# Gate and up column pairs of an FFN computed token-major, their h turned by DMA

## The chip, the cores and the metric

One core of a Trainium2 chip (trn2) runs the whole program in one launch. The metric is the device time of a launch in microseconds (us); the kernel before takes 912.5 us (median of three runs, 911.65 to 912.99).

## The reference

Two decoder layers work on 256 tokens of width 1024. Each layer is an FFN, a mixer and a second FFN, each between two RMSNorms, with the result added to the residual. Only the FFN is touched by the change:

```python
def _rmsnorm(x, g):
    x32 = x.astype(jnp.float32)
    y = x32 * lax.rsqrt(jnp.mean(x32 * x32, axis=-1, keepdims=True) + RMS_EPS)
    return y.astype(x.dtype) * g

def _swiglu(h, wg, wu, wd):
    return (jax.nn.silu(h @ wg) * (h @ wu)) @ wd
...
for l in range(DEPTH):
    f = _swiglu(_rmsnorm(h, ff1_norm_pre[l]), ff1_w_gate[l], ff1_w_up[l], ff1_w_down[l])
    h = h + 0.5 * _rmsnorm(f, ff1_norm_post[l])
    m = _hybrid_mixer(...)
    h = h + _rmsnorm(m, mix_norm_post[l])
    f = _swiglu(_rmsnorm(h, ff2_norm_pre[l]), ff2_w_gate[l], ff2_w_up[l], ff2_w_down[l])
    h = h + 0.5 * _rmsnorm(f, ff2_norm_post[l])
```

The FFN's hidden width is 2816, everything is float32.

## The kernel before

**Arithmetic.** A float32 product runs on TensorE as three products: each operand x is split into hi, rounded to the format fp32r (ScalarE, lines L114 for weights and L250 for activations), and lo = x - hi (VectorE, L115 and L251), and hi·hi + lo·hi + hi·lo is summed in PSUM. `xT` holds the normed input turned, that is with the 1024 features on partitions in eight blocks `k` and the 256 tokens on the free axis; `both` holds its hi and lo side by side. t is the tile of 128 tokens, 0 or 1.

**Units.** The 2816 hidden columns are eleven units of 256, numbered 0 to 10. Units 0 and 1 are `FIRST`; (2, 3), (5, 6) and (8, 9) are `QUADS`, computed together by a scheme with seven products; 4, 7 and 10 are `PAIRS`, computed one at a time by `ffn_pair`. There are four FFNs, so twelve pairs. After a unit's hidden activation h has been made and turned (`hT`), its share of the down projection is `down(i, t)`: twelve matmuls of 512 columns into the two PSUM banks `acc[t]` (L412), for t = 0 and t = 1. I write (10, 0) for `down` of unit 10 and tile 0. Of the last four units (7 to 10, `TAIL`) the t = 0 parts come first and the t = 1 parts after them, so that the norms of tile 0 run while TensorE does tile 1.

**A pair before.** `ffn_pair` calls `mm_side` for gate and then for up. Weights stand still and the input streams: the result is feature-major, so h needs no turning. For each half j of 128 features, eight matmuls stream `both`, 512 columns (L359), and eight stream hi alone, 256 columns, with the weights' lo (L361); so a pair is 32 matmuls of 512 columns and 32 of 256. ScalarE copies the second half of the bank out (L364), VectorE adds the first (L365), four times a pair; then silu (L541), the product (L544) and the split of h (L250, L251).

**The other units** are token-major: the input stands still, the weights stream 512 columns (L390, L559), and h comes out with tokens on partitions. To turn it, `send` parts the float32 words into 16-bit halves (ScalarE, L510) and issues a DMA transpose on SyncE's queue (L514), and `receive` joins them again (ScalarE, L522) and splits them (L250, L251). In some places `turn_tile` turns on TensorE instead (L533). Within a pair, `turn()` receives one tile of the quad before it and `take()` the other.

**End of an FFN.** `post(0)` norms acc[0] and adds it to h (ScalarE L258 and L260, GpSimd L263, VectorE L275 and L282); `pre_scale` norms h for the next stage (L258, L260, L263, L291), and `pre_turn` turns the result on TensorE, two times four transposes (L301). The last FFN has nothing after it but the output. Weights come by DMA on SyncE's queue (L85) into five raw buffers, and are split into five pairs of hi and lo buffers. `pump()` loads and splits ahead as buffers allow; `W.allowed` limits how many loads it may issue.

**Order.** The program is recorded in the order of the code, and the framework then sets each engine's own order by its estimates of when things are ready; `issue_after` and `keep_in_program_order` bind it. All engines but TensorE's weight loads run their queue strictly in that order.

## Time and profile before

| | |
|---|---|
| Timed runs, median (lowest, highest) | 912.5 (911.65, 912.99) us |
| Profiled execution, span on the chip | 910.8 us |
| Granted TensorE clock, mean | 0.999 |
| DMA: bytes moved, mean rate | 198.63 MB, 218 GB/s |
| Packets under 512 B | 35858 of 60880 |

The profiled execution is given by its span, first to last instruction; the timed runs' median lies 1.7 us above it. Busy times are unions, so that overlapping instructions count once; a row of a group gives the line, the engine, the operation, the tiles it writes and reads, the count, then busy us and the mean ns of one, then idle time before it with its releaser. PE is TensorE, ACT ScalarE, DVE VectorE, POOL GpSimd, SP SyncE. A matmul's own duration of 0.39 us overlaps the next; what counts is the spacing from one start to the next.

### The profile page before, as it was taken

How to read it: one execution, taken by the hardware profiler on the slowest of the kernel's cores; microseconds unless marked ns; L12 is line 12 of the kernel's file. 1: busy time of each engine (PE TensorE's matmuls, PEld its weight loads, DVE VectorE, ACT ScalarE, POOL GpSimd, SP SyncE). 2: the span in 40 equal slices, each digit the busy share in tenths (PEclk: the TensorE clock that was granted, in tenths of full speed). 3: DMA queues.
4: the chain of work that ended last, by engine and by line, in shares of the span. 5: the costliest groups of instructions: out<-in, count | busy, mean ns of one | idle time of the engine just before them, and what ended most of it. 6: DMA issues, size and time to landing. Idle time of an engine off the chain costs nothing.

```text
span 910.8 us, 12262 instructions
## 1 busy us (share of the span) xinstructions
PE 901.0 (99%) x4556; PEld 760.6 (84%) x4556; DVE 801.6 (88%) x1068; ACT 665.9 (73%) x1045; POOL 29.8 (3%) x49
## 2 busy tenths in 40 slices
PE   8999999999999999999999999999999999999997
PEld 5888888889988888888888888888998888888885
DVE  6999988789878999988899999988989699999983
ACT  7776776778858777776878768767797668768772
POOL 0000000000001000000000000000000110000000
PEclk9999999999999999999999999999999999999999
DMA  9677977765355587768755968695824256978641
GB/s 360 181 274 227 384 188 282 251 214 204 78 195 208 128 314 205 289 162 288 244 187 149 339 196 299 173 305 200 298 109 162 93 173 180 323 214 298 177 124 47
DMA packets 60880, 198.63 MB, mean 218 GB/s; under 512 B 35858, under 2 KB 36370, under 8 KB 38804
## 3 DMA queue, kind: packets, MB, share of 16 engines
q1 hardware_dynamic: 58948, 185.13, 58.5%
q0 software_dynamic: 1728, 12.58, 7.3%
q8 instruction: 36, 0.59, 0.2%
q14 instruction: 24, 0.20, 0.1%
q10 hardware_dynamic: 144, 0.13, 0.0%
HBM read 188.65 MB, written 1.05 MB: 208 GB/s over the span
## 4 chain that ended last, share of the span: by engine, by line
PE 92%; DVE 5%; issue 2%; DMA 1%; ACT 0%; POOLq 0%; SPq 0%; POOL 0%; DVEq 0%
PE acc L412 29%; PE wk L559 23%; PE wk L390 13%; PE wk L359 9%; PE wk L350 6%; PE wk L361 5%; DVE lo L115 3%; PE wk L377 1%; PE wk L301 1%; DMA raw<-in_ff_f 1%; PE wk L1084 1%; PE acc L827 0%; DVE raw L113 0%; PE acc L897 0%; PE acc L1032 0%
## 5 line engine op out<-in xcount | busy, mean ns | idle before, releaser
L115 DVE TENSOR_TENSOR lo<-raw,hi 128x1024 fp32r<-128x1024 f32 (+2 forms) x452 | 464.3, 1076 | 37.4 <-ACT hi L114 36.8
L114 ACT ACTIVATE hi<-raw 128x1024 fp32r<-128x1024 f32 (+2 forms) x452 | 398.7, 937 | 72.2 <-DVE raw L113 30.1
L412 PE MATMUL acc<-hi,t 128*128 128x512 f32 x832 | 214.7, 391 | 0.0
L412 PEld LDWEIGHTS acc<-hi,t 128*128 128x128 f32 x832 | 155.0, 188 | 31.4
L412 PE MATMUL acc<-lo,t 128*128 128x512 f32 x416 | 113.4, 390 | 0.0
L559 PE MATMUL wk<-hi,n 128*128 128x512 f32 x384 | 100.5, 390 | 0.0
L390 PE MATMUL wk<-hi,xT 128*128 128x512 f32 x384 | 98.9, 393 | 0.2
L359 PE MATMUL wk<-xT,hi 128*128 128x512 f32 x384 | 95.9, 392 | 0.0
L412 PEld LDWEIGHTS acc<-lo,t 128*128 128x128 f32 x416 | 77.9, 188 | 16.3
L390 PEld LDWEIGHTS wk<-hi,xT 128*128 128x128 f32 x384 | 71.0, 188 | 16.4 <-ACT hi L114 1.6
L559 PEld LDWEIGHTS wk<-hi,n 128*128 128x128 f32 x384 | 71.8, 188 | 14.8
L359 PEld LDWEIGHTS wk<-xT,hi 128*128 128x128 f32 x384 | 69.8, 189 | 13.0
L559 PE MATMUL wk<-hi,xT 128*128 128x512 f32 x288 | 77.6, 390 | 0.1
L113 DVE TENSOR_TENSOR raw<-raw,raw 128x1024 f32<-128x1024 f32 x56 | 67.2, 1215 | 0.0
L559 PEld LDWEIGHTS wk<-hi,xT 128*128 128x128 f32 x288 | 53.8, 188 | 11.3 <-DVE t L599 0.4
L361 PEld LDWEIGHTS wk<-xT,lo 128*128 128x128 f32 x384 | 52.4, 190 | 3.8
L361 PE MATMUL wk<-xT,lo 128*128 128x256 f32 x384 | 53.5, 282 | 0.0
L559 PE MATMUL wk<-lo,n 128*128 128x512 f32 x192 | 52.1, 390 | 0.0
L390 PE MATMUL wk<-lo,xT 128*128 128x512 f32 x192 | 52.0, 391 | 0.0
L510 ACT ACTIVATE t<-t 128x1024 uint16<-128x1024 uint16 x31 | 32.6, 1055 | 24.4 <-DVE t L630 16.2
L390 PEld LDWEIGHTS wk<-lo,xT 128*128 128x128 f32 x192 | 36.0, 188 | 8.3 <-DVE lo L115 0.8
L559 PEld LDWEIGHTS wk<-lo,n 128*128 128x128 f32 x192 | 36.0, 188 | 7.7 <-DVE lo L115 0.2
(184 smaller groups left out, 947.8 us busy)
## 6 DMA issues: line engine op xcount, KB each, us to landing
raw<-in_ff_q SPq DMA_DIRECT2D x48, 1024.0 KB, 6.4
raw<-in_ff_d SPq DMA_DIRECT2D x44, 1024.0 KB, 5.1
raw<-in_ff_f SPq DMA_DIRECT2D x16, 1024.0 KB, 7.1
raw<-in_ff_q POOLq DMA_DIRECT2D x12, 1024.0 KB, 8.0
raw<-in_ff_g SPq DMA_DIRECT2D x12, 1024.0 KB, 4.8
raw<-in_ff_u SPq DMA_DIRECT2D x12, 1024.0 KB, 4.8
raw<-in_w_in SPq DMA_DIRECT2D x10, 1024.0 KB, 5.3
raw<-in_w_kvz SPq DMA_DIRECT2D x8, 1024.0 KB, 6.1
```

The lines of the kernel that those rows point to most:

```text
L113: nc.vector.tensor_tensor(raw[:, s], self.raw[x][:, s], self.raw[y][:, s], op=op)
L114: self.act = nc.scalar.activation(hi[:, s], raw[:, s], AF.Copy)
L115: nc.vector.tensor_tensor(lo[:, s], raw[:, s], hi[:, s].bitcast(F32), op=ALU.subtract)
L301: pre_turn.last = nc.tensor.transpose(ps[:, k * P : (k + 1) * P], xn[i][:, k * P : (k + 1) * P], ident)
L350: nc.tensor.matmul(ps, w[:, k, s], y[:, k, :], start=i == 0 and k == 0, stop=i == 2 and k == KD - 1)
L359: nc.tensor.matmul(ps, hi[:, k, s], both[:, :, k, :], start=k == 0, stop=k == KD - 1)
L361: mm_side.end = nc.tensor.matmul(ps[:, S:], lo[:, k, s], xT[0][:, k, :], start=False, stop=k == KD - 1, skip_group_check=True)
L377: nc.tensor.matmul(ps, x[:, k, s], w[:, k, :], start=i == 0 and k == 0, stop=i == 2 and k == KD - 1)
L390: m = nc.tensor.matmul(ps, y[:, k, :], w[:, k, :], start=h == 0 and n == 0, stop=h == 1 and n == len(parts) - 1)
L412: m = nc.tensor.matmul(acc[b], x[:, j, s], w[:, j, b * 512 : (b + 1) * 512], start=first and j == 0 and i == 0, stop=last and j == 1 and i ...
L510: part = send.last = nc.scalar.activation(halves.rearrange("p (a n) -> p a n", a=2), x[:, :].bitcast(U16).rearrange("p (n a) -> p a n", a= ...
L559: nc.tensor.matmul(ps, x[:, k, :], w[:, k, :], start=first and n == 0, stop=n == len(parts) - 1, skip_group_check=not first)
```

## The change

A pair becomes token-major like the rest. Its weights are stored as two units of half of K each, with the 256 columns of gate and the 256 of up side by side. `half(k, t)` is twelve matmuls of 512 columns; the order is half 0 of both tiles, half 1 of tile 0, half 1 of tile 1, into two PSUM banks, one a tile. After `half(0, 1)` comes `turn()`, after `half(1, 0)` comes `take()`. Silu now reads the gate half of the bank and the product the up half. Then h is sent and received by DMA. For pairs 4 and 7 both tiles go in one transpose, which is received in `turn()` of the next quad. For pair 10 each tile has its own h, its own send of half the size and its own receive behind the pair; meanwhile `W.allowed = 0` holds loads back until the second of them has been issued. `send`, `receive` and the slicing in `mm_rows` take their size from the tile.

```diff
         def pair(i):
-            for k in "gu":
-                p[k, i] = W.plan(a[f"ff{n}_{k}"][l, PAIRS.index(i)])
+            for k in range(2):
+                p["p", i, k] = W.plan(a[f"ff{n}_p"][l, 2 * PAIRS.index(i) + k])
...
-    def ffn_pair(i, p, turn, take, by_dma):
-        s = mm_side(p["g", i], buf())
-        taken = mm_side.last
-        nc.scalar.activation(s, s, AF.Silu)
-        turn()
-        hf = mm_side(p["u", i], buf(), take)
-        nc.vector.tensor_tensor(hf, hf, s, op=ALU.mult)
-        hT = (buf(F32R), buf(F32R))
-        split_into(hT, (slice(None), slice(None)), hf)
-        if by_dma:
-            pump_behind(taken)
-        else:
-            W.pump()
-        return hT
+    def ffn_pair(i, p, turn, take):
+
+        by_tile = i == PAIRS[-1]
+        ps = [bank(), bank()]
+        hf = [buf(n=256) for _ in range(2)] if by_tile else buf()
+        sent = []
+
+        def half(k, t):
+            hi, lo = (w[:, :UNIT].rearrange("p (k n) -> p k n", k=4) for w in W.get(p["p", i, k]))
+            x = [y[:, 4 * k : 4 * k + 4, t * P : (t + 1) * P] for y in xT]
+            parts = [(c, n) for n in range(3) for c in range(4)]
+            for n, (c, part) in enumerate(parts):
+                y, w = ((x[0], hi), (x[0], lo), (x[1], hi))[part]
+                m = nc.tensor.matmul(ps[t], y[:, c, :], w[:, c, :], start=k == 0 and n == 0,
+                                     stop=k == 1 and n == len(parts) - 1)
+            return m
+
+        def gated(t):
+            s = buf(n=256)
+            nc.scalar.activation(s, ps[t][:, :256], AF.Silu)
+            if by_tile:
+                nc.vector.tensor_tensor(hf[t], ps[t][:, 256:], s, op=ALU.mult)
+                sent.append(send(hf[t]))
+            else:
+                s, u, o = (x.rearrange("p (j n) -> p j n", n=P) for x in (s, ps[t][:, 256:], hf))
+                nc.vector.tensor_tensor(o[:, t::2], u, s, op=ALU.mult)
+
+        half(0, 0)
+        mid = half(0, 1)
+        W.done(p["p", i, 0])
+        with tc.issue_after(mid.ins):
+            turn()
+        half(1, 0)
+        take()
+        gated(0)
+        ffn_pair.end = half(1, 1)
+        W.done(p["p", i, 1])
+        gated(1)
+        if not by_tile:
+            sent.append(send(hf))
+        if by_tile:
+            W.allowed = 0
+        pump_behind(mid)
+        if by_tile:
+            W.allowed = 10**6
+            pump_behind(send.dma)
+        return sent
...
             def turn():
+                if sent:
+                    hT[before[0]] = receive(sent.pop())
                 if not hf:
                     return
...
-        for b in before:
-            both(b)
+        hT[NU - 1] = {0: receive(sent[0]), "at": 0}
+        both(NU - 1)
         post(0, acc[0], gain, before_next if last else None)
         xn0 = None if last else before_next(0)
+        hT[NU - 1][1] = receive(sent[1])
         for i in range(NU - TAIL, NU):
```

How the orders move, at three places. `hi41` and `lo41` are the down weights of unit 10 in the first FFN, `hi36` those of unit 7, `hi40` those of unit 9; acc62 and acc63 are acc[0], acc64 and acc65 acc[1]. L412 of before is L393 now.

TensorE at the end of the first FFN, before: (9, 0) ends, then one matmul of (7, 1) and the twelve of (10, 0).

```order
L412 MATMUL acc63_507<-hi40_1387,t125_1450 128x512
L412 MATMUL acc65_521<-hi36_1306,t107_1143 128x512
L412 MATMUL acc62_506<-hi41_1503,t132_1499 128x512 x2
L412 MATMUL acc62_506<-lo41_1504,t132_1499 128x512 x2
L412 MATMUL acc62_506<-hi41_1503,t133_1500 128x512 x2
L412 MATMUL acc63_507<-hi41_1503,t132_1499 128x512 x2
L412 MATMUL acc63_507<-lo41_1504,t132_1499 128x512 x2
L412 MATMUL acc63_507<-hi41_1503,t133_1500 128x512 x2
L412 MATMUL acc64_520<-hi36_1306,t107_1143 128x512
L412 MATMUL acc65_521<-hi36_1306,t107_1143 128x512
```

Now, same place (the rows before these are six more of (7, 1), behind the end of (9, 0)):

```order
L393 MATMUL acc64_520<-lo36_1273,t113_1203 128x512
L393 MATMUL acc65_521<-lo36_1273,t113_1203 128x512
L393 MATMUL acc64_520<-hi36_1272,t114_1204 128x512
L393 MATMUL acc62_506<-hi41_1451,t141_1497 128x512 x2
L393 MATMUL acc62_506<-lo41_1452,t141_1497 128x512 x2
L393 MATMUL acc62_506<-hi41_1451,t142_1498 128x512 x2
L393 MATMUL acc63_507<-hi41_1451,t141_1497 128x512 x2
L393 MATMUL acc63_507<-lo41_1452,t141_1497 128x512 x2
L393 MATMUL acc63_507<-hi41_1451,t142_1498 128x512 x2
L393 MATMUL acc65_521<-hi36_1272,t114_1204 128x512
```

Nine matmuls of (7, 1) stand in front of (10, 0) now, and three are left behind it. The second and third FFN end alike; in the fourth (10, 0) follows the twenty-four of (8, 0) and (9, 0) at once, as before.

TensorE at the transposes of `pre_turn`, first FFN, before: they come when (9, 1) is done. wk152 and wk153 are the two banks they fill, n150 and n151 the halves of the normed input.

```order
L412 MATMUL acc64_520<-hi40_1387,t130_1476 128x512
L412 MATMUL acc65_521<-hi40_1387,t130_1476 128x512
L301 MATMUL wk152_1629<-ident_82,n150_1589 128x128 x4
L301 MATMUL wk153_1636<-ident_82,n151_1590 128x128 x4
L412 MATMUL acc64_520<-hi41_1503,t132_1499 128x512 x2
```

Now:

```order
L393 MATMUL acc64_520<-hi40_1353,t133_1422 128x512
L393 MATMUL acc65_521<-hi40_1353,t133_1422 128x512
L393 MATMUL acc64_520<-hi41_1451,t162_1549 128x512 x2
L301 MATMUL wk164_1589<-ident_82,n159_1543 128x128 x4
L393 MATMUL acc64_520<-lo41_1452,t162_1549 128x512
L301 MATMUL wk165_1596<-ident_82,n160_1544 128x128 x4
```

Two matmuls of (10, 1) have slid in front of the first four transposes, one more in front of the second four. Between the last matmul of (10, 0) and the first transpose there stand 29 matmuls now (3, 24 and 2), 34 before.

ScalarE behind the weight splits in the last pair of the fourth FFN, before. t888 and t893 are joined halves of quad (8, 9), tiles 0 and 1; L364, L541 are the copies and the silu of the pair.

```order
L522 ACTIVATE t888_8152<-t882_8062 128x2x512
L114 ACTIVATE hi195_8208<-raw159_8025 128x1024
L250 ACTIVATE t889_8154<-t888_8152 128x512
L114 ACTIVATE hi195_8208<-raw159_8025 128x1024
L541 ACTIVATE t885_8112<-t885_8112 128x512
L364 ACTIVATE t891_8158<-wk892_8159 128x256
L522 ACTIVATE t893_8178<-t884_8080 128x2x512
L364 ACTIVATE t891_8158<-wk896_8184 128x256
L250 ACTIVATE t894_8180<-t893_8178 128x512
L250 ACTIVATE t897_8204<-t891_8158 128x512
```

Now, from the join of tile 1 on (L505 is `receive`, L540 the silu, L492 the parting in `send`, L250 the split; t927 and t928 are the h of the two tiles, t937 and t940 what the DMA turned, t941 and t953 what is joined from it):

```order
L505 ACTIVATE t932_8004<-t924_7926 128x2x512
L250 ACTIVATE t933_8006<-t932_8004 128x512
L540 ACTIVATE t935_8010<-wk925_7958 128x256
L492 ACTIVATE t936_8013<-t927_7960 128x512
L540 ACTIVATE t938_8029<-wk926_7959 128x256
L492 ACTIVATE t939_8032<-t928_7961 128x512
L505 ACTIVATE t941_8066<-t937_8015 128x2x256
L250 ACTIVATE t942_8068<-t941_8066 128x256
L505 ACTIVATE t953_8104<-t940_8034 128x2x256
L250 ACTIVATE t954_8106<-t953_8104 128x256
```

The pair's four copies and its silu are gone; silu of tile 0 stands behind both joins of the quad's tiles, and behind it come two partings and two more joins with their splits, ahead of the norm of acc[0] (L258).

More of the change, by code (lines that the diff above doesn't have):

```diff
@@ L350, in mm_feat @@
                 nc.tensor.matmul(ps, w[:, k, s], y[:, k, :], start=i == 0 and k == 0, stop=i == 2 and k == KD - 1)
-    def mm_side(u, out, between=None):
-        hi, lo = (w[:, :UNIT].rearrange("p (k n) -> p k n", k=KD) for w in W.get(u))
-        for j in range(2):
-            s = slice(j * P, (j + 1) * P)
-            ps = bank()
-            for k in range(KD):
-                nc.tensor.matmul(ps, hi[:, k, s], both[:, :, k, :], start=k == 0, stop=k == KD - 1)
-            for k in range(KD):
-                mm_side.end = nc.tensor.matmul(ps[:, S:], lo[:, k, s], xT[0][:, k, :], start=False, stop=k == KD - 1,
-                                               skip_group_check=True)
-            o = out[:, j * S : (j + 1) * S]
-            nc.scalar.activation(o, ps[:, S:], AF.Copy)
-            mm_side.last = nc.vector.tensor_tensor(o, ps[:, :S], o, op=ALU.add)
-            if between and not j:
-                between()
-        W.done(u)
-        return out
     def mm_tok(ps, u, t, ncols=256):
@@ L402, in mm_rows @@
             s = slice(None)
-            xh, xl = (x.rearrange("p (j n) -> p j n", j=4)[:, xs["at"] : xs["at"] + 2] for x in xs[t])
+            xh, xl = (x.rearrange("p (j n) -> p j n", n=P)[:, xs["at"] : xs["at"] + 2] for x in xs[t])
         else:
@@ L507, in send @@
     def send(x, more=False):
-        halves = buf(U16, 1024)
+        n = 2 * x.shape[1]
+        halves = buf(U16, n)
         part = send.last = nc.scalar.activation(halves.rearrange("p (a n) -> p a n", a=2),
                                     x[:, :].bitcast(U16).rearrange("p (n a) -> p a n", a=2), AF.Copy)
-        turned = buf(U16, 1024)
+        turned = buf(U16, n)
         with tc.issue_after(part.ins):
-            t = nc.sync.dma_start_transpose(turned.rearrange("p (a n) -> p a n", a=8), halves)
+            t = send.dma = nc.sync.dma_start_transpose(turned.rearrange("p (a n) -> p a n", n=P), halves)
         if W.allowed < 10 and not more:
@@ L519, in receive @@
     def receive(turned):
-        x = buf()
+        n = turned.shape[1] // 2
+        x = buf(n=n)
         nc.scalar.activation(x[:, :].bitcast(U16).rearrange("p (n a) -> p a n", a=2), turned.rearrange("p (a n) -> p a n", a=2),
                              AF.Copy)
-        hT = (buf(F32R), buf(F32R))
+        hT = (buf(F32R, n), buf(F32R, n))
         split_into(hT, (slice(None), slice(None)), x)
@@ L536, in turn_tile @@
         return hT
-    def ffn_pair(i, p, turn, take, by_dma):
-        s = mm_side(p["g", i], buf())
-        taken = mm_side.last
-        nc.scalar.activation(s, s, AF.Silu)
-        turn()
-        hf = mm_side(p["u", i], buf(), take)
-        nc.vector.tensor_tensor(hf, hf, s, op=ALU.mult)
-        hT = (buf(F32R), buf(F32R))
-        split_into(hT, (slice(None), slice(None)), hf)
-        if by_dma:
-            pump_behind(taken)
-        else:
-            W.pump()
-        return hT
+    def ffn_pair(i, p, turn, take):
[41 more added lines that the diff above has]
+        return sent
     def product(ps, left, job, first):
@@ L672, in both @@
                 down(i, 0, behind)
-        before = list(FIRST)
+        before, sent = list(FIRST), None
         for i in range(2, NU):
@@ L703, in ffn @@
             if i in PAIRS:
-                hT[i] = ffn_pair(i, p, turn, take, by_dma)
-                u = mm_side.end.ins
+                sent = ffn_pair(i, p, turn, take)
+                u = ffn_pair.end.ins
                 for b in before:
@@ L711, in ffn @@
                               two(i))
-                before = [i, i + 1]
+                sent, before = None, [i, i + 1]
             if later and i in PAIRS:
@@ L1278, in _layout @@
         d[f"ff{n}_f"] = np.concatenate([half(g[:, :, :512]), half(u[:, :, :512])], axis=1)
-        d[f"ff{n}_g"] = cols(g)[:, PAIRS]
-        d[f"ff{n}_u"] = cols(u)[:, PAIRS]
+        d[f"ff{n}_p"] = np.concatenate([half(np.concatenate([x[:, :, i * 256 : (i + 1) * 256] for x in (g, u)], axis=2))
+                                        for i in PAIRS], axis=1)
         d[f"ff{n}_q"] = quads(g, u)
```

## The prediction

> **What bounds the kernel now.** I first read the profile's page, its busy times and its chain of waits, with shares of the span.
>
> ```profile
> PE 901.0 (99%) x4556; PEld 760.6 (84%) x4556; DVE 801.6 (88%) x1068; ACT 665.9 (73%) x1045; POOL 29.8 (3%) x49
> ...
> PE 92%; DVE 5%; issue 2%; DMA 1%; ACT 0%; POOLq 0%; SPq 0%; POOL 0%; DVEq 0%
> ```
>
> TensorE is busy 901.0 of 910.8 us and 92% of the chain. So an edit counts in two ways: by how long TensorE's instructions run, and by any idle time that it opens or closes in TensorE's queue. Work on another engine counts only where TensorE comes to wait for it.
>
> Next the table of stretches, cut to three pairs from first to last matmul. Its columns are the stretch, its length, then busy time and count of PE, PEld, DVE, ACT and POOL, the granted clock, the DMA share and GB/s. The first row is unit 7 of the first FFN, the second unit 10 of the first FFN, the third unit 10 of the fourth.
>
> ```profile
> 113.67:124.82 11.15, 11.15 (x66) 9.83 (x65) 8.96 (x11) 8.89 (x12) 0.00 (x0) 1.00 0.87 263
> 157.48:168.63 11.15, 11.15 (x66) 9.83 (x64) 10.20 (x11) 11.15 (x15) 0.00 (x0) 1.00 1.08 321
> 874.20:885.35 11.15, 11.15 (x66) 9.83 (x64) 9.49 (x11) 11.15 (x15) 0.00 (x0) 1.00 0.23 40
> ```
>
> Each pair takes TensorE 11.15 us at a granted clock of 1.00. In the last pair of an FFN ScalarE is as full as TensorE: 11.15 of 11.15. DMA is full in the first FFN's last pair (1.08) and nearly free in the fourth's (0.23), where no weights are left to load.
>
> **A, the matmuls.** The chain of waits in that region gives runs of matmuls with start, length and count.
>
> ```profile
> 102.95 10.88 PE wk L559 x48
> 113.83 1.81 PE wk L359 x8
> 115.65 0.95 PE wk L361 x8
> 116.60 1.84 PE wk L359 x8
> ```
>
> A pair is 32 matmuls of 512 columns (L359) and 32 of 256 (L361) and becomes 48 of 512 that read two tensors in token-major form, which is just what L559 does in a quad: x48 in 10.88 us, 0.2267 us each. L361 takes 0.95/8 = 0.119 each. The streamed columns are the same, 24576, so the gain is only 11.15 - 10.88 = 0.27 us a pair, and 12 pairs make **-3.24 us**. All of it is on TensorE's path.
>
> **B, one stall.** In the first pair of the first FFN TensorE idles. The fences are the stretch from the pair's first matmul to the one after its last (columns as above), TensorE's instruction behind the gap, and VectorE's that releases it.
>
> ```profile
> 65.84:78.28 12.44, 11.77 (x69) 10.27 (x68) 12.38 (x16) 8.94 (x13) 0.00 (x0) 1.00 0.98 342
> ```
>
> ```profile
> 72.23 0.63 PE L533 MATMUL wk<-ident,t 128*128 128x128 f32 x4 [0.67 <-DVE t L630]
> ```
>
> ```profile
> 71.40 0.68 DVE L630 TENSOR_TENSOR t<-wk,t 128x512 f32<-128x512 f32 x1
> ```
>
> The 12.44 us hold a pair of 11.15 and four transposes. Four start-to-start spacings of 128x128 are about 0.43 (eight take 0.79 in the rows under C), so the stall is worth 0.86. The transposes stand behind 28 matmuls of the new pair, at 65.84 + 28 x 0.2267 = 72.19, and their input is ready at 71.40 + 0.68 = 72.08. The stall goes; I book **-0.8 us**, as the two times lie only 0.1 apart. The next waiter, the second half of the pair's weights, is split two weight units ahead of L630 in VectorE's queue and isn't late.
>
> **C, a new wait before the next stage's transposes.** At the end of an FFN with a successor, the norm of tile 0 runs while TensorE does tile 1. These rows are the chain in the first FFN.
>
> ```profile
> 176.82 1.07 PE L412 MATMUL acc<-hi,t 128*128 128x512 f32 x4
> ...
> 184.99 1.04 PE L301 MATMUL wk<-ident,n 128*128 128x128 f32 x8
> 185.78 0.47 PE L412 MATMUL acc<-hi,t 128*128 128x512 f32 x1
> ```
>
> ```profile
> 177.47 0.60 ACT L258 ACTIVATE n<-acc 128x512 bf16<-128x512 f32 x1 [0.29 <-PE acc L412]
> ...
> 182.61 3.74 ACT L114 ACTIVATE hi<-raw 128x512 fp32r<-128x512 f32 x7
> ```
>
> ```profile
> 183.68 1.41 DVE L291 SCALAR_TENSOR_TENSOR n<-h,s,gains 128x512 f32<-128x512 f32 x2 [0.44 <-POOL s L263]
> ```
>
> The last matmul of (10, 0) starts at T = 176.82 + 0.23 = 177.05; its end releases L258 at 177.47. The first half of L291 is done about 0.75 after 183.68, so the chain takes 184.43 - 177.05 = 7.38 us. Before, 35 spacings led from T to the transposes: 35 x 0.2267 = 7.94, no wait. Now (7, 1) has been moved in front of (10, 0), and 30 spacings lead there: 6.80. VectorE has five splits of 128x512 ahead of L291 now; at an estimated 0.6 each (L251 under D has that size and 0.685 with overlap) they should just fit into its idle time ahead of that line. TensorE waits 7.38 - 6.80 = 0.58, with a hop between engines some 0.65, and everything behind it with it. Three FFNs have this end: **+1.95 us**. Between zero, if ScalarE and GpSimd pass the chain on sooner, and 0.8 each is possible. The matmuls moved forward aren't lost: they are the cover that D needs.
>
> **D, the turned h of unit 10.** Before, unit 10's h came feature-major and needed two splits. Now tile 0 goes through silu, product, parting, DMA, join and split before (10, 0). First ScalarE in the fourth FFN, then the durations of the pieces, from the groups by form.
>
> ```profile
> 880.48 0.63 ACT L364 ACTIVATE t<-wk 128x256 f32<-128x256 f32 x2
> 881.00 1.38 ACT L522 ACTIVATE t<-t 128x1024 uint16<-128x1024 uint16 x1
> 882.23 1.05 ACT L114 ACTIVATE hi<-raw 128x1024 fp32r<-128x1024 f32 x1
> 883.16 0.64 ACT L250 ACTIVATE t<-t 128x512 fp32r<-128x512 f32 x1
> 883.68 1.07 ACT L114 ACTIVATE hi<-raw 128x1024 fp32r<-128x1024 f32 x1
> 884.63 0.63 ACT L541 ACTIVATE t<-t 128x512 f32<-128x512 f32 x1
> ```
>
> ```profile
> L510 ACT ACTIVATE t<-t 128x1024 uint16<-128x1024 uint16 x31 | 32.6, 1055 | 24.4 <-DVE t L630 16.2 <-DVE t L620 7.6 <-DVE t L477 0.6
> L251 DVE TENSOR_TENSOR t<-t,t 128x512 fp32r<-128x512 f32 x41 | 28.1, 685 | 2.6 <-ACT t L250 1.9
> L365 DVE TENSOR_TENSOR t<-wk,t 128x256 f32<-128x256 f32 x48 | 18.7, 416 | 1.7 <-ACT t L364 1.7
> L1060 ACT ACTIVATE t<-t 128x512 uint16<-128x512 uint16 x8 | 5.3, 767 | 1.3 <-PE acc L1032 1.3
> L250 ACT ACTIVATE t<-wk 128x256 fp32r<-128x256 f32 x8 | 3.0, 369 | 3.2 <-DVE t L251 3.2
> ```
>
> From 880.48, without the copies (L364), I lay the spacings of these rows in the new order: join 1.23, split of weights 0.93, L250 0.52, split of weights 0.95, join 1.23, giving 885.34; the second L250 ends at 885.98. VectorE's L251 (0.69), then the product (0.42 as L365) end at 887.1; silu of tile 0 lies beside them. A parting of half size is 1055/2 and a bit, 0.6: 887.7. Now the DMA. The transposes in the trace are all of full size; the first row is a quiet stretch of the second FFN, the next a crowded one, the last SyncE's own time for issuing (min/median/max ns).
>
> ```profile
> t<-t SPq DMA_TRANSPOSE x2, 3.0
> ...
> t<-t SPq DMA_TRANSPOSE x2, 5.6
> ```
>
> ```profile
> L514 SPq DMA_TRANSPOSE t<-t x2: 1232/1232/1232, 872.6 to 874.9; - x2
> ```
>
> Of 3.0 us to landing 1.23 is the issue. If all of it halves, half the size lands in 1.5, if nothing does in 3.0; I take **2.5**, as if the issue alone halved. Then h lands at 890.25, is joined (0.77, L1060) and split (0.37, L250) at 891.4. TensorE asks for it at 874.20 + 10.88 + 24 x 0.2267 = 890.52: a wait of **0.9**. In the first three FFNs nine matmuls of (7, 1), 2.04 us, stand in front as well, which move the need from 890.5 to 892.6 in these terms; but there ScalarE also has four pieces of the next stage's weights, 0.53 each (3.74/7 in L114's row under C), that can't start before the pair ends, ahead of the parting. The two nearly cancel, so I book **0.1 each**. D is 0.9 + 0.3 = **+1.2 us**.
>
> The Trainium skill, "DMA: Bandwidth & Descriptors", under "Anatomy of one DMA", fits a DMA issued through GpSimd as about 2.0 us fixed plus bytes over 436 GB/s. As an estimate by that page, half of 256 KB saves 0.3 us, so 2.7 to landing, and the sum would be some 0.8 us higher. No run here shows a half-size transpose, and these are issued by SyncE, so it decides nothing.
>
> **At nothing.** ScalarE loses four copies (369 ns) and a silu (623) a pair and gains two smaller silus, a parting and a join; in pairs 4 and 7 h is wanted only after many matmuls of the next quad. VectorE loses four additions (416). With that cover gone the join's 1.38 us (L522) would show. `W.allowed = 0` holds back only loads that the next stage wants tens of us later. On SyncE's queue one transpose more a pair, two in pair 10, 1.2 us at most each, stands ahead of loads that are early.
>
> **Sum.** -3.24 - 0.8 + 1.95 + 1.2 = -0.9 on the profiled 910.8, so 909.9. The median of the timed runs is 912.5, 1.7 above the profiled execution: **911.6 us**. A measurement of this kernel can tell about 0.2%, 1.8 us, from no change: 910.7 to 914.3. Its own range: transposes of 2.3 to 2.8 us (-0.8 to +1.2) and C between 0.4 and 0.8 each (-0.75 to +0.45), 910.1 to 913.2. Chance 0.52, of which 0.10 lies below 910.7.
>
> **Rivals.**
>
> *The waits C and D stay away*, because ScalarE, freer in every pair, runs ahead of my row-by-row count. Then -4.04 stands alone: **908.5 us**, faster. For it: ScalarE loses work in each pair, and 0.6 and 0.9 are small against chains of 7 and 17 us. Against it: C's chain doesn't start earlier by that, and D is bound by the DMA. Chance 0.24.
>
> *The half-size transposes land late*, slower than before. Each 0.1 us beyond 2.5 costs 0.1 at four ends, because (10, 0) heads TensorE's queue and everything stands behind it. From 3.2 us on the sum passes 914.3; at 3.5 it is **915.6**; at the crowded row's 5.6 it is 911.6 + 4 x 3.1 = 924. For it: the first three FFNs' ends have full DMA (share 1.08). Against: the loads are held until the second transpose is issued, and the last one ahead of them is issued well before.
>
> ```profile
> 165.36 9.51 SPq L85 DMA_DIRECT2D raw<-in_w_in  x3
> ```
>
> ```profile
> raw<-in_w_in SPq DMA_DIRECT2D x10, 1024.0 KB, 5.3
> ```
>
> The first of these three (SyncE's instructions, then the page's median to landing) is the last load ahead of them; 165.36 + 5.3 is 170.7, and the transposes come at about 172. Chance 0.16.
>
> *The new matmuls gain less.* L359's second run of eight under A takes 1.84, 0.230 each. At that spacing a pair of 48 is 11.04 us, 12 x 0.11 = 1.3 are saved instead of 3.24, and the result is **913.5**, no change. The Trainium skill, "TensorE: Matmul & The Clock Gate", under "Back-to-back issue gap", speaks against the gain too: a single matmul's gap is N/2.4 + 2.5 ns, so two of 256 cost 2.5 ns more than one of 512, and by that page a pair would save 0.04 us, the sum would be +1.9. The trace differs: two of L361 take 0.2375, one of L559 0.2267, 11 ns apart. Chance 0.08.
>
> **The numbers.** Faster: 0.10 + 0.23 = 0.33. Same: 0.42 of the forecast, 0.01 of the first rival, 0.07 of the third: 0.50. Slower: 0.16 and 0.01 of the third, 0.17. The range goes from the first rival's 908.5, a little less for its own spread, to 914.5, where the late transposes begin to count: 908.3 to 914.5 leaves out about 0.2.
>
> **What the new profile would show.** A right: pairs of 10.88 us from first to last matmul. B: no idle time of TensorE before the transposes in the first pair. C: some 0.6 us before L301 in three FFNs, released by L291. D: 0.9 us before (10, 0) in the fourth FFN, released by L250, and at most 0.3 in the others; half-size transposes landing after 2.5 us. It is wrong if pairs take 11.0 or more, if transposes take over 3 us, or if TensorE waits somewhere that isn't named here.

## The result, and the profile after

The changed kernel takes 923.21 us (921.86 to 925.34, four runs) against 912.49 us (911.65 to 912.99) for the kernel before: a ratio of 1.0119, 95% interval 1.0107 to 1.0131. Its profiled execution spans 922.1 us against 910.8. The forecast was 911.6, range 908.3 to 914.5. It was wrong: the kernel is slower by 1.2%, where no change that can be measured was the likeliest case. One execution is left out of the figures: the fourth of run e5 below, which took 2588 us, and nothing on record says why.

First the page: busy times, then the chain of waits by engine.

```profile
PE 901.6 (98%) x4364; PEld 750.4 (81%) x4364; DVE 786.8 (85%) x1036; ACT 679.3 (74%) x1045; POOL 32.6 (4%) x49
...
PE 74%; DVE 9%; ACT 9%; issue 4%; DMA 3%; POOL 0%; POOLq 0%; DVEq 0%; SPq 0%; ACTq 0%
```

TensorE's busy time has hardly moved (901.0 before); its share of the chain has fallen from 92% to 74%. The time went into waiting. The table of waits says where; its columns are line and releaser, total us, times, longest us.

```profile
PE acc L393 <- ACT t L250: 7.8, 5, 2.5
PE wk L301 <- DVE n L291: 2.6, 3, 0.9
...
PE wk L575 <- DVE t L615: 0.6, 1, 0.6
...
PE wk L575 <- DVE wk L603: 0.2, 1, 0.2
```

The 7.8 us are (10, 0) waiting for the turned h of unit 10 in four FFNs (and 0.23 once for (8, 0)), that is D. The 2.6 us are the next stage's transposes waiting for the norm, C. Two small waits in the quad (8, 9) of the first FFN are new (L575 is the quads' matmul). TensorE's rows show one D of the first FFN and one C, and the worst D, in the fourth:

```profile
178.22 0.73 PE L393 MATMUL acc<-hi,t 128*128 128x512 f32 x2 [1.57 <-ACT t L250]
...
188.64 0.66 PE L301 MATMUL wk<-ident,n 128*128 128x128 f32 x4 [0.83 <-DVE n L291]
```

```profile
900.29 0.77 PE L393 MATMUL acc<-hi,t 128*128 128x512 f32 x2 [2.50 <-ACT t L250]
900.86 1.05 PE L393 MATMUL acc<-lo,t 128*128 128x512 f32 x2
901.71 1.91 PE L393 MATMUL acc<-hi,t 128*128 128x512 f32 x4
903.41 1.02 PE L393 MATMUL acc<-lo,t 128*128 128x512 f32 x2
904.27 1.54 PE L393 MATMUL acc<-hi,t 128*128 128x512 f32 x6
```

Behind the 2.50 us of idling, eight matmuls stand 0.43 apart (among them the four from 901.71 on), then the spacing is 0.23 again. The stretches show the clock beside the pairs (stretch, length, five engines, granted clock, DMA share, GB/s):

```profile
112.63:123.51 10.88, 10.88 (x49) 9.01 (x48) 8.80 (x10) 8.37 (x9) 0.00 (x0) 1.00 0.88 239
881.29:892.17 10.88, 10.88 (x50) 8.96 (x48) 8.28 (x8) 10.12 (x13) 0.00 (x0) 1.00 0.27 55
896.00:906.00 10.00, 7.50 (x26) 5.68 (x26) 2.32 (x5) 5.83 (x13) 0.00 (x0) 0.83 0.14 27
```

Pairs take 10.88 us now, as forecast. Behind the long wait the granted clock is 0.83.

By spacings of TensorE's starts the bill is as follows. A gap is the time from one start to the next, and the normal 0.23 us is taken off each.

| Term | Measured on | us |
|---|---|---|
| A | twelve pairs of 10.88 for 11.15 | -3.24 |
| B | first pair with its transposes, 12.44 before, 11.43 now | -1.0 |
| D | gaps of 1.95, 2.37, 1.94 and 2.88 | +8.2 |
| Fallen clock | eight matmuls, 0.2 each | +1.6 |
| C | gaps of 1.22, 1.22 and 1.28 | +3.0 |
| First FFN, quad (8, 9) and (8, 0) | gaps of 0.61, 1.01 and 0.62 | +1.55 |

That is +10.1 of the 11.3 us between the two spans; the rest is scattered in small gaps.

So what had to be explained was D: 8.2 us and a fallen clock where 1.2 had been booked. ScalarE's rows in the fourth FFN, of the kernel before and of the changed one, show that the DMA is not it:

```profile
874.78 5.79 ACT L114 ACTIVATE hi<-raw 128x1024 fp32r<-128x1024 f32 x6
```

```profile
883.50 5.79 ACT L114 ACTIVATE hi<-raw 128x1024 fp32r<-128x1024 f32 x6
889.19 1.36 ACT L505 ACTIVATE t<-t 128x1024 uint16<-128x1024 uint16 x1
...
895.95 0.63 ACT L492 ACTIVATE t<-t 128x512 uint16<-128x512 uint16 x1 [0.82 <-DVE t L542]
...
899.01 0.77 ACT L505 ACTIVATE t<-t 128x512 uint16<-128x512 uint16 x1 [1.04 <-DMA t<-t]
899.82 0.42 ACT L250 ACTIVATE t<-t 128x256 fp32r<-128x256 f32 x1
```

```profile
t<-t SPq DMA_TRANSPOSE x2, 2.4
```

The half-size transposes (last fence, DMA issues of a stretch in the first FFN, median to landing) land after 2.4 us; 2.5 was assumed. But the six weight splits start 2.2 us behind the pair's start (881.29), where they started 0.6 behind it before (874.78 against 874.20), and everything after them is late by that 1.6: the parting (L492) starts 3.8 us behind the pair's end at 892.17, where 887.1 - 885.1 = 2.0 had been reckoned. ScalarE came late to the last pair. The experiments ask why.

### The profile page after: what moved, and what is told of

Its sections match the earlier page's. It is cut to its first block, busy times and chain, and to the rows that moved or that the text cites. A ratio compares the mean times of both kernels' runs of the same rounds, so it can differ in the third digit from the quotient of the medians.

```text
span 922.1 us, 11889 instructions
## 1 busy us (share of the span) xinstructions
PE 901.6 (98%) x4364; PEld 750.4 (81%) x4364; DVE 786.8 (85%) x1036; ACT 679.3 (74%) x1045; POOL 32.6 (4%) x49
## 3 DMA queue, kind: packets, MB, share of 16 engines
HBM read 188.65 MB, written 1.05 MB: 206 GB/s over the span
## 4 chain that ended last, share of the span: by engine, by line
PE 74%; DVE 9%; ACT 9%; issue 4%; DMA 3%; POOL 0%; POOLq 0%; DVEq 0%; SPq 0%; ACTq 0%
PE acc L393 21%; PE wk L575 19%; PE wk L371 13%; PE wk L534 9%; PE wk L350 6%; DVE lo L115 5%; ACT hi L114 4%; ACT t L505 2%; PE wk L358 1%; DMA t<-t 1%; DMA raw<-in_ff_q 1%; PE wk L301 1%; DMA raw<-in_ff_f 1%; PE wk L1103 1%; ACT t L250 1%
## 5 line engine op out<-in xcount | busy, mean ns | idle before, releaser
L115 DVE TENSOR_TENSOR lo<-raw,hi 128x1024 fp32r<-128x1024 f32 (+2 forms) x452 | 465.4, 1076 | 50.4 <-ACT hi L114 49.7
L114 ACT ACTIVATE hi<-raw 128x1024 fp32r<-128x1024 f32 (+2 forms) x452 | 398.9, 936 | 77.1 <-DVE raw L113 33.0
L393 PE MATMUL acc<-hi,t 128*128 128x512 f32 x832 | 216.0, 392 | 7.8 <-ACT t L250 7.8
L393 PEld LDWEIGHTS acc<-hi,t 128*128 128x128 f32 x832 | 156.0, 189 | 42.3 <-ACT t L250 9.9
L393 PE MATMUL acc<-lo,t 128*128 128x512 f32 x416 | 115.3, 393 | 0.0
L575 PE MATMUL wk<-hi,n 128*128 128x512 f32 x384 | 100.6, 391 | 0.2 <-DVE wk L603 0.2
L371 PE MATMUL wk<-hi,xT 128*128 128x512 f32 x384 | 98.9, 393 | 0.4 <-ACT hi L114 0.3
L534 PE MATMUL wk<-hi,xT 128*128 128x512 f32 x384 | 96.8, 389 | 0.0
L393 PEld LDWEIGHTS acc<-lo,t 128*128 128x128 f32 x416 | 78.4, 189 | 16.2
L492 ACT ACTIVATE t<-t 128x1024 uint16<-128x1024 uint16 (+1 forms) x47 | 46.2, 984 | 53.7 <-DVE t L646 28.2
L371 PEld LDWEIGHTS wk<-hi,xT 128*128 128x128 f32 x384 | 70.9, 188 | 16.7 <-ACT hi L114 1.8
L534 PEld LDWEIGHTS wk<-hi,xT 128*128 128x128 f32 x384 | 72.1, 188 | 15.0
L575 PEld LDWEIGHTS wk<-hi,n 128*128 128x128 f32 x384 | 71.7, 188 | 15.4 <-DVE wk L603 0.6
L575 PE MATMUL wk<-hi,xT 128*128 128x512 f32 x288 | 77.2, 390 | 0.7 <-DVE t L615 0.6
L575 PEld LDWEIGHTS wk<-hi,xT 128*128 128x128 f32 x288 | 53.9, 188 | 12.5 <-issue 1.0
L505 ACT ACTIVATE t<-t 128x1024 uint16<-128x1024 uint16 (+1 forms) x43 | 54.0, 1256 | 6.2 <-DMA t<-t 6.2
L371 PE MATMUL wk<-lo,xT 128*128 128x512 f32 x192 | 52.1, 391 | 0.0
L575 PE MATMUL wk<-lo,n 128*128 128x512 f32 x192 | 52.0, 389 | 0.0
L534 PE MATMUL wk<-lo,xT 128*128 128x512 f32 x192 | 51.4, 390 | 0.0
L251 DVE TENSOR_TENSOR t<-t,t 128x512 fp32r<-128x512 f32 (+1 forms) x45 | 28.7, 638 | 17.6 <-ACT t L250 17.6
```

The source lines that it names most:

```text
L114: self.act = nc.scalar.activation(hi[:, s], raw[:, s], AF.Copy)
L115: nc.vector.tensor_tensor(lo[:, s], raw[:, s], hi[:, s].bitcast(F32), op=ALU.subtract)
L251: split_into.lower = nc.vector.tensor_tensor(lo, src_f32, hi.bitcast(F32), op=ALU.subtract)
L371: m = nc.tensor.matmul(ps, y[:, k, :], w[:, k, :], start=h == 0 and n == 0, stop=h == 1 and n == len(parts) - 1)
L393: m = nc.tensor.matmul(acc[b], x[:, j, s], w[:, j, b * 512 : (b + 1) * 512], start=first and j == 0 and i == 0, stop=last and j == 1 and i ...
L492: part = send.last = nc.scalar.activation(halves.rearrange("p (a n) -> p a n", a=2), x[:, :].bitcast(U16).rearrange("p (n a) -> p a n", a= ...
```

## The experiments

Two theories stood at first. Backlog: the h of units 4 and 7 is now joined and split inside the quad that follows, and that makes ScalarE and VectorE late. Unit 10 alone: its own parting, transfer and join behind a full ScalarE are enough. In all runs the rest of the program is that of the changed kernel unless said otherwise.

**e1, unit 7 back in the old form.** The old code stays beside the new, with a list of the units that use it (the host lays their weights out as before):

```diff
+                if i in OLD:                       # OLD = (7,)
+                    hT[i], sent = old_pair(i, p, turn, take), None
+                    u = mm_side.end.ins
+                else:
+                    sent = ffn_pair(i, p, turn, take)
+                    u = ffn_pair.end.ins
```

> Only unit 7's pair goes back to the old feature-major form in all four FFNs; units 4 and 10 stay token-major. Theory 1 (backlog): unit 7's h, joined and split inside the quad (8, 9), makes ScalarE and VectorE reach the last pair 1.6 to 2.0 us later than before, and that lateness goes straight into the wait of (10, 0). Then the parting of unit 10's tile 0 starts about 2.2 us behind the pair's last matmul in the fourth FFN (3.8 in the changed kernel) and 3.0 in the first (5.0), the two stalls of 0.4 and 0.8 us in the first FFN's quad (8, 9) go, the fourth FFN waits about 1 us without a drop of the clock, and waits for h plus waits for the norm come to about 1 us an FFN in the other three: span about 913. Theory 2 (unit 10 alone): parting, DMA and join of unit 10 behind a full ScalarE are the whole wait; the parting keeps its 3.8 and 5.0 us, and the span is 922 to 923.

917.75 us, ratio 1.0063 (1.0048 to 1.0078), span 917.2. A split verdict. In the first FFN the parting came 3.2 us behind the pair's end (169.58 against 166.36) and the quad's stalls were gone, as the backlog theory said. In the fourth it still came 3.6 us behind (890.87 against 887.27), the gap was 2.73 (an idle time of 2.35), and the clock fell again. There the lateness had another source.

**e2, unit 10 back in the old form** (`OLD = (10,)`).

> Only unit 10's pair goes back to the old form; units 4 and 7 stay token-major. Both theories: no wait in front of (10, 0) or of the next stage's transposes, since h of unit 10 needs no turning. Eight pairs save 0.27 each (2.2) and the stall in the first pair stays away (1.0): span about 908 if unit 7 costs nothing (theory 2), about 909 to 911 if the backlog in the quad (8, 9) still holds TensorE there, 1.3 us in the first FFN at least (theory 1).

913.13 us, ratio 1.0007 (0.9997 to 1.0016), span 911.5. C is gone, D all but gone, and with them the slowdown, yet A and B don't show up in the time: the first FFN keeps its stalls in the quad (8, 9) (gaps of 0.56 and 1.05), (8, 0) waits in the first and third FFN (gaps of 0.78 and 0.61), and in all four a gap of 0.4 to 0.5 stands behind the 24th matmul after the pair. So units 4 and 7 give back what they gain, even where nothing waits for unit 10.

**e3, unit 10 turned on TensorE.**

```diff
-                sent.append(send(hf[t]))
+                sent.append(hf[t])
...
-        hT[NU - 1] = {0: receive(sent[0]), "at": 0}
+        hT[NU - 1] = {0: turn_half(sent[0]), "at": 0}     # two transposes into a bank, split
...
-        hT[NU - 1][1] = receive(sent[1])
+        with tc.issue_after(done.ins):                    # done: last matmul of (10, 0)
+            hT[NU - 1][1] = turn_half(sent[1])
```

> All pairs stay token-major, but unit 10's h is turned on TensorE (two transposes of 128x128 a tile, four an FFN) in place of parting, DMA and join; loads are not held back. The chain from product to split loses a parting (0.6), a transfer (2.4) and a join (0.8). Both theories of the backlog expect the waits in front of (10, 0) to fall under 0.5 us, the clock to stay up, and (10, 0) to stand ahead of most of (7, 1) again, so that the wait for the norm goes too: 922.1 - 8.7 - 1.7 - 3.2 + 1.7 for the transposes is a span of about 910. If the waits have another cause than the length of this chain, the span stays above 915.

911.86 us, ratio 1.0003 (0.9993 to 1.0012), span 911.4. The waits of C and D are gone: the table of TensorE's waits has nothing over 0.3 us of them. The chain from product to split is what they hung on; the quad (8, 9) (waits of 0.7 and 0.2) and small gaps again take the gain of the rest.

**e4, empty matmuls in the fourth FFN's wait.**

```diff
+        if last:
+            fill = bank()
+            with tc.issue_after(down.last.ins):           # behind (9, 0)
+                for _ in range(11):
+                    tc.keep_in_program_order(nc.tensor.matmul(fill, zeros[:, :P], zeros, start=True, stop=True))
         both(NU - 1)
```

> The changed kernel with eleven empty matmuls of 512 columns put on TensorE behind (9, 0) in the fourth FFN, into the 2.66 us in which it idles; nothing else moves. If the spacing of 0.43 us of the eight matmuls behind that wait is a clock that fell in the idle time, they come at 0.23 now and the span falls by 1.6 to 920.5. If they are slow because operands come late, nothing changes: 922.1, or 0.2 more.

```profile
898.15 2.32 PE L739 MATMUL wk<-zeros 128*128 128x512 bf16 x10
900.61 0.73 PE L393 MATMUL acc<-hi,t 128*128 128x512 f32 x2
901.17 0.62 PE L393 MATMUL acc<-lo,t 128*128 128x512 f32 x2
901.63 1.08 PE L393 MATMUL acc<-hi,t 128*128 128x512 f32 x4
```

921.3 us, ratio 1.0091 (1.0070 to 1.0112), span 920.7. The trace has ten of the eleven empty matmuls. (10, 0) waits as long as before, but behind it the matmuls stand 0.23 apart and the granted clock is 1.00: the slow eight were a clock that fell because TensorE had idled. The span fell by 1.4 us, about their 1.6, but that alone would show little: four spans of the changed kernel lie between 920.1 and 923.6, and other gaps of this execution moved by up to 0.8.

**e5, (7, 1) in front of (10, 0) in the fourth FFN.**

```diff
+        if last:
+            down(NU - TAIL, 1)
+            W.done(p["d", NU - TAIL])
-        both(NU - 1)
+        both(NU - 1, down.last.ins if last else None)
```

> The changed kernel with the twelve matmuls of (7, 1) put in front of (10, 0) in the fourth FFN, where nothing follows that the norm of tile 0 could hold up. They fill 2.72 us, the wait there is 2.66. Theory: wait (2.65) and fallen clock (1.65) both go, and nothing else changes: span 922.1 - 4.3 = 917.8. Were the wait made by TensorE's own order behind it, h would come later by as much as the matmuls take, and the span would stay near 922.

919.25 us (median of three), span 915.9, ratio 1.0074 (1.0057 to 1.0091). No gap in front of (10, 0) and no slow matmul in that FFN. The fall in the span is larger than the 4.3 us expected because the profiled execution was also 1.7 us ahead by the last pair of the first FFN, with nothing changed there; the two others have spans of 917.5 and 918.2. The fourth FFN's share is as expected. TensorE's own order is not the cause of the wait, it decides whether the wait is covered.

**e6, units 4 and 7 in the old form** (`OLD = (4, 7)`).

> Units 4 and 7 in the old form, only unit 10 token-major. Theory (backlog from both quads): in the fourth FFN the quad (5, 6) already ran late after unit 4, its loads are queued behind its transposes, so the backlog outlived unit 7's return to the old form. With both back, the parting of unit 10's tile 0 starts 2.2 to 2.7 us behind the pair's end in the fourth FFN (3.8 in the changed kernel, 3.6 with unit 7 alone put back) and about 3 in the first, (10, 0) of the fourth FFN waits about 1 us without a drop of the clock, the waits of an end come to about 1 us in the others, and the span is 910.8 - 1.1 + 4 = 914. If the lateness is unit 10's own, the fourth FFN keeps 3.6 to 3.8 us and a wait over 2.4 with the fallen clock, span about 917.

915.43 us, ratio 1.0040 (1.0026 to 1.0054), span 913.2. The first transpose of unit 10 is issued 13.46 us behind the pair's start in the fourth FFN (15.31 in the changed kernel, 15.13 in e1), the wait is 0.8 and the clock stays up. So the lateness is not unit 10's own.

**e7, unit 4 alone in the old form** (`OLD = (4,)`).

> Only unit 4 in the old form, 7 and 10 token-major. Theory: in the fourth FFN the loads behind the transposes of quad (5, 6) are issued 1.5 us sooner, about 5.2 us after the start of unit 7's pair as in the kernel before (6.7 in the changed kernel), and of the 1.6 us of backlog at the last pair about 1 goes: parting 2.8 us behind the pair's end, a wait under 2 without the fallen clock. The first FFN has its stall of 0.9 in the first pair again and 1.1 us less gain from the matmuls, so the span is 920 to 921. If unit 7 alone made the lateness, the parting keeps its 3.8 us and the span is about 924.

914.12 us, ratio 1.0023 (1.0013 to 1.0032), span 912.4: 9 us come back by unit 4 alone, far more than expected. TensorE's waits, then its wait in the fourth FFN:

```profile
PE wk L302 <- DVE n L292: 3.1, 4, 0.9
...
PE acc L394 <- ACT t L251: 0.7, 1, 0.7
```

```profile
891.94 0.73 PE L394 MATMUL acc<-hi,t 128*128 128x512 f32 x2 [0.67 <-ACT t L251]
```

With unit 7 and unit 10 both token-major, D is a gap of 1.06, 0.83 more than normal, in the fourth FFN and nothing in the others, the parting starts 1.9 us behind the pair's end, and the quad (8, 9) of the first FFN has no stall. That is the D of the prediction. SyncE's queue shows what unit 4 changes (fourth FFN; rows of the kernel before, of the changed kernel, of e7):

```profile
831.38 4.10 SPq L514 DMA_TRANSPOSE t<-t  x2
835.58 0.52 SPq L85 DMA_DIRECT2D raw<-in_ff_q  x1
836.20 0.38 SPq L85 DMA_DIRECT2D raw<-in_ff_d  x1
```

```profile
840.27 4.10 SPq L496 DMA_TRANSPOSE t<-t  x2
844.47 0.53 SPq L85 DMA_DIRECT2D raw<-in_ff_q  x1
```

```profile
832.26 4.10 SPq L497 DMA_TRANSPOSE t<-t  x2
836.46 0.52 SPq L86 DMA_DIRECT2D raw<-in_ff_q  x1
```

The pair of unit 7 starts at 830.39, 837.77 and 831.26. So the transposes of the quad (5, 6) are issued 1.0, 2.5 and 1.0 us behind it, and the loads, which that quad holds back until then, at 5.2, 6.7 and 5.2. The reason stands in the quad itself (ScalarE and VectorE of the changed kernel):

```profile
817.02 1.35 ACT L505 ACTIVATE t<-t 128x1024 uint16<-128x1024 uint16 x1
818.24 1.03 ACT L114 ACTIVATE hi<-raw 128x1024 fp32r<-128x1024 f32 x1
819.17 0.62 ACT L250 ACTIVATE t<-t 128x512 fp32r<-128x512 f32 x1
```

```profile
819.30 1.23 DVE L115 TENSOR_TENSOR lo<-raw,hi 128x1024 fp32r<-128x1024 f32 x1 [1.23 <-ACT hi L114]
820.45 0.68 DVE L251 TENSOR_TENSOR t<-t,t 128x512 fp32r<-128x512 f32 x1
```

Unit 4's join (L505) and split (L250) stand among the weight splits (L114). VectorE waits 1.23 us for the split behind the join, then has 0.68 of its own to do for h. It has hardly any slack from there to the end of the quad, so its last sums, the parting and the transposes come 1.5 us late. Some 40 us later, in the quad (8, 9), ScalarE waits for a load, and VectorE behind it:

```profile
858.06 4.85 ACT L114 ACTIVATE hi<-raw 128x1024 fp32r<-128x1024 f32 x5 [2.94 <-DMA raw<-in_ff_q]
```

```profile
859.15 3.50 DVE L115 TENSOR_TENSOR lo<-raw,hi 128x1024 fp32r<-128x1024 f32 x3 [2.77 <-ACT hi L114]
...
868.25 0.68 DVE L251 TENSOR_TENSOR t<-t,t 128x512 fp32r<-128x512 f32 x1
```

This load is not one of the two that were held back: the one issued at 844.47 has landed 5.7 us later, at 850.1. It is one that GpSimd issues (L119; it adds into a raw buffer, so work of ScalarE and VectorE on the quad comes first); it lands 8.1 us later, at 858.0. Its issue, before and in the changed kernel:

```profile
841.96 0.86 POOL L119 DMA_DIRECT2D raw<-in_ff_q  x1 [47.21 <-ACT hi L114]
```

```profile
849.87 0.86 POOL L119 DMA_DIRECT2D raw<-in_ff_q  x1 [48.13 <-ACT t L250]
```

Before, ScalarE's wait was 2.25 us and ended at 849.96, 24.2 us ahead of the last pair; now it ends 23.2 ahead, 1.0 us later. From there on VectorE has no idle time up to the first product of the quad (L646), and unit 7's split (L251 at 868.25) holds it up by 0.6 more. Together that is the 1.6 us seen above.

**e8, the quad (5, 6) holds no loads back.** If the loads held back carry the lateness on, freeing them must help though the transposes stay late.

```diff
-            W.allowed = int(i == QUADS[0])
+            W.allowed = 1 if i == QUADS[0] else 10**6
```

> The changed kernel, with the two loads that the quad (5, 6) holds back until its transposes are issued let go at once; all else as it was. Theory: these loads carry the lateness of quad (5, 6) into quad (8, 9), so ScalarE's wait of 2.9 us for them in the fourth FFN falls to under 2, and the last pair starts with a backlog smaller by about 1 us (parting 2.8 behind the pair's end, no fallen clock): span about 919. Rival: the transposes, now next to loads, land after 5 us in place of 3 and make TensorE wait in the pair of unit 7; the parting keeps its 3.8 us and the span is 922 or more.

914.60 us, ratio 1.0026 (1.0015 to 1.0036), span 913.3. The loads are issued 0.8 and 3.9 us behind the pair's start, the transposes still at 2.5; in the quad (8, 9) of the fourth FFN ScalarE's wait falls from 2.94 to 0.94 us, the first transpose of unit 10 is issued 13.14 us behind the pair's start in place of 15.31, D is 0.5. The rival's first half came true, the transposes of the quad land after 6.5 and 7.0 us, but TensorE does not wait for them in the pair of unit 7. What is left is C, a gap of 2.77 in the first FFN among it, where the order of the matmuls came out differently and the clock fell once more.

One line that touches neither unit 4 nor unit 10 gives 8.6 us back, so the hold is a condition of the slowdown. That the held loads themselves carry the lateness is not shown: the load for which ScalarE waits is GpSimd's. And the edit also changed ScalarE's order. In the changed kernel the first parting of the quad (8, 9) (880.23) waits for VectorE ahead of the silu L635 (881.20), and the second parting stands behind both; here L635 comes first and the two partings follow at once. Of the 2.2 us by which ScalarE reaches the last pair's splits sooner, VectorE's earlier product (L646, 2.6 us ahead of the pair in place of 1.8) makes 0.8; the rest goes with that order.

**e9, weight splits behind the norm** (on e7):

```diff
-        W.pump(SPLIT_BUFS - 1)
+        with tc.issue_after(scaled0.ins):                 # last multiply of pre_scale(0)
+            W.pump(SPLIT_BUFS - 1)
```

> The kernel with unit 4 alone put back, plus one order: the weight splits of the next stage wait until the norm of tile 0 has been multiplied out. In that kernel GpSimd's power, 0.56 us long where VectorE is idle, takes up to 1.2 where VectorE splits weights beside it, and ends 0.4 us behind VectorE's last split. Theory: the two engines hold each other up there, so without splits the power takes 0.6, the chain to the transposes is 7.2 us, and the three gaps of 1.2 to 1.3 us from the last matmul to the transposes fall to 0.6 to 0.8: span 912.4 - 1.7 = 910.7, if the later splits cost the mixer nothing. Rival: the power takes as long as it takes, the gaps stay at 1.2 to 1.3, and late splits only add: span 912.4 or more.

918.75 us, ratio 1.0067 (1.0051 to 1.0082), span 918.1. The chain did as expected, the kernel didn't. GpSimd's power at the norm of tile 0 in the first FFN: its second instruction in the kernel before, then both of the changed kernel and of e9.

```profile
182.78 0.86 POOL L263 TENSOR_TENSOR s<-s,halfexp 128x1 f32<-128x1 f32 x1 [3.65 <-ACT s L260]
```

```profile
182.37 0.56 POOL L263 TENSOR_TENSOR s<-s,halfexp 128x1 f32<-128x1 f32 x1 [56.93 <-ACT s L260]
186.59 1.21 POOL L263 TENSOR_TENSOR s<-s,halfexp 128x1 f32<-128x1 f32 x1 [3.65 <-ACT s L260]
```

```profile
182.09 0.56 POOL L264 TENSOR_TENSOR s<-s,halfexp 128x1 f32<-128x1 f32 x1 [57.17 <-ACT s L261]
186.30 0.55 POOL L264 TENSOR_TENSOR s<-s,halfexp 128x1 f32<-128x1 f32 x1 [3.65 <-ACT s L261]
```

Without splits beside it the second power takes 0.55 in place of 1.21, and the gaps in front of the transposes fell to 0.79 and 0.91 in the second and third FFN (1.22 and 1.28 in e7). In the first, whose rows these are, the gap did not fall (1.38, 1.32 in e7); what took the gain there was not tried. But the late splits make the mixer wait, gaps of 0.6 to 1.05 in five places, and the first FFN had a D of 1.5 again, behind a wait of ScalarE for a load of 5.0 us (2.8 in e7). That load is again GpSimd's: it lands after 10.1 us, and after 10.3 in the first FFN of the changed kernel, where it takes 8.0 in e7 and before. So the first FFN can come late without unit 4, and why the load is slow there was not tried.

**e10, unit 10 on TensorE and no hold.** e3 and e8 together, and four matmuls of (7, 1) fixed between the transposes and (10, 0), eight behind:

```diff
+        with tc.issue_after(turn_half.last.ins):
+            m = mm_rows(acc[1], p["d", NU - TAIL], 1, hT[NU - TAIL], False, False, span=(0, 4))
-        both(NU - 1)
+        both(NU - 1, m.ins)
```

> The changed kernel with both mended: unit 10's h is turned on TensorE, four matmuls of (7, 1) stand between those transposes and (10, 0) and the other eight behind it, and the quad (5, 6) holds no loads back. Theory: no wait in front of (10, 0) or of the norm's transposes over 0.3 us, none in the quad (8, 9) of the first FFN; 910.8 - 3.2 - 1.0 + 1.7 for sixteen transposes and some 0.6 of small gaps is a span of about 909, and the time is 0.1 to 0.2% under the kernel before. If letting the loads go crowds the transposes of the quads, stalls of 1 us or more show up in the pairs of unit 7 and the time is that of the kernel before or above it.

```profile
PE acc L225 <- DVE zeros L214: 2.3, 1, 2.3
PE wk L301 <- DVE n L291: 0.2, 1, 0.2
```

910.48 us (909.70 to 910.85), ratio 0.9981 (0.9972 to 0.9989), span 908.8. Both rows of TensorE's waits lie before 12 us, at the start of the program, and stand so in the kernel before. No other wait is left, and the kernel is a little faster than both.

**e11, a join and split added to the kernel before.**

```diff
             def turn():
+                if i == QUADS[1]:
+                    receive(hT[PAIRS[0]][0][:, :].bitcast(U16))
```

It adds work to each quad (5, 6) whose result nothing reads.

> The kernel before, all pairs in the old form, with one join and split of 128x512 added in each quad (5, 6), where the changed kernel has them for unit 4; their result is used by nothing. Theory: this alone makes the quad late. Its two transposes are issued 2.4 and 5.3 us after the start of unit 7's pair (1.0 and 3.9 in the kernel before), the loads behind them at 6.6 (5.2), and TensorE has a stall of about 1 us in the quad (8, 9) of the first FFN or in front of (8, 0); span 911 to 912.5, since no wait of unit 10 stands behind it here. Rival: the lateness comes from the new pair's own instructions; transposes and loads stay at 1.0, 3.9 and 5.2.

912.57 us, ratio 1.0003 (0.9994 to 1.0013), span 910.4.

```profile
832.18 4.10 SPq L514 DMA_TRANSPOSE t<-t  x2
836.37 0.53 SPq L85 DMA_DIRECT2D raw<-in_ff_q  x1
```

The pair of unit 7 starts at 829.82 here: transposes at 2.36, loads at 6.55 (2.5 and 6.7 in the changed kernel), and much the same in all four FFNs. The join alone makes the quad late, without any token-major pair. ScalarE's splits in the last pair of the fourth FFN show how far that reaches:

```profile
875.47 5.78 ACT L114 ACTIVATE hi<-raw 128x1024 fp32r<-128x1024 f32 x6
```

They start 1.8 us behind the pair's first matmul (873.64), where it was 0.6 in the kernel before and 2.2 in the changed one: one join and split in the quad (5, 6) make 1.2 of the 1.6 us. In the second and third FFN the run is 1.3 and 1.2 us late, in the first 0.6, where the changed kernel is 2.9 late. The stall expected in the first FFN did not come, and the time is that of the kernel before: lateness costs nothing as long as no one waits for it.

## Why the prediction was wrong, point by point

- **A** was right: 10.88 us a pair. **B** was right: the stall is gone, -1.0 for -0.8.
- **"At nothing" is the step that failed**, where it says that in pairs 4 and 7 "h is wanted only after many matmuls of the next quad". TensorE indeed didn't wait for that h. But a join and a split entered two queues in the middle of a quad in which VectorE has no slack, the quad's transposes went 1.5 us late, and ScalarE came 1.6 us late to the last pair of the fourth FFN. I looked at who reads the moved result and not at who stands behind the moving instruction. e11 shows 1.2 us of this lateness from the join and split alone, e7 that it is gone without unit 4's, e8 that late transposes do little harm without the hold. How it gets from the late transposes to GpSimd's load is read from the traces and was not tried by itself; in the first FFN the slow landing of that load is part of it and stays unexplained.
- **D** had the right working and a wrong start. It took ScalarE's start from the trace of before, and laid the rest of the chain from there. With a start much as before (e7) the wait is 0.83 for 0.9, and nothing in the other FFNs for 0.1 each. The transpose was right too, 2.4 for 2.5, though by luck (last section). In the changed kernel the start is 1.6 us late in the fourth FFN, 2.9 in the first and 1.5 in the two between, and since (10, 0) had no slack, nearly all of it became waiting: 2.65 in the fourth for 0.83. A fallen clock, which the prediction did not have, added 1.6.
- **C** was right in place and releaser and too small: 1.0 for 0.65 each. The term that was mis-sized is the chain of 7.38 us, which measures 7.79 in the first FFN. Nearly all of the difference is the power on GpSimd, 1.21 in place of the 0.86 in the trace of before, since VectorE's five splits, which I let "just fit" into the idle time, lay beside it.
- Of the rivals, late transposes had the right sign and not the mechanism: they land in 2.4 us, with the loads held. Rivals one and three did not happen.
- The range was too narrow for one reason: every bound in it was a size of C or D, and none asked what a late quad would cost.

## What to carry to other kernels

Work that is moved off the busiest engine's path still lands in some queue: list for each new instruction what stands behind it on its own engine, and whether a hold or a transfer is tied to that. A term of a forecast that starts from a time in the trace of before is only as good as that start; ask first what in the change can shift it. And a wait at the head of the busiest engine's queue passes on every microsecond of lateness upstream, so a short route there (here two transposes in place of a transfer) is worth more than the fraction of a microsecond that the new shape saves.

## What the runs showed of the hardware

- TensorE's clock fell after an idle time of 2.5 us (spacing 0.43 for eight matmuls, 3.4 us, granted clock 0.83 over ten us), and again after 2.35 us in e1; after waits of up to 2.0 us in the other FFNs it didn't. In the changed kernel the granted clock goes to 0.50 only 0.55 us behind the end of the idle time; in e8, in front of the first FFN's transposes, it goes down 2.0 us into an idle time of 2.39. So the length of the wait alone does not decide. The Trainium skill, "TensorE: Matmul & The Clock Gate", section "Part 1: The HAM clock gate", has the clock halve after an idle window of about 3.4 us that runs freely, and come back after a busy window as long. The halving and the 3.4 us of slow matmuls agree; here idle times of 2.35 to 2.5 us were enough.
- GpSimd's power of one column takes 0.55 us, and up to 1.2 where VectorE subtracts one SBUF operand from another beside it (L115); it then ends 0.4 us behind VectorE's instruction. Beside L275, which reads one operand from PSUM, it stays at 0.55. The Trainium skill, "SBUF — State Buffer", section "SBUF: two separate sides", says that a VectorE operation with two SBUF inputs shuts out a GpSimd operation that reads SBUF; the trace agrees.
- A transpose of half the size takes SyncE as long to issue (1.19 us for 1.23) and lands after 2.4 us in place of 3.0 (one in the second FFN after 3.1). The guess that the issue alone would halve gave the right sum for a wrong reason.
